# A chunked delta rule: inverses from blocks of 16 and a scan with its coefficients computed ahead

## Chip, cores and metric

The kernel runs on one core of a Trainium2 chip. The metric is device time in microseconds (us), the median of several runs. Five engines work from their own instruction queues: TensorE (PE, with its weight loads as PEld), VectorE (DVE), ScalarE (ACT), GpSimd (POOL) and SyncE (SP), which issues most DMAs.

## What is computed

Two blocks of two layers each act on 512 tokens of width 1024. The change touches the second block only, and in each of its two layers only the gated delta rule: 6 heads of width 64, run forwards and backwards over the tokens, in 8 chunks of 64 tokens. For each direction and head the reference does this:

```python
A = where(strict, einsum("bhncd,bhnsd->bhncs", kb, kc) * decay, 0)   # 64 x 64 in each chunk
u, w = triangular_solve(I + A, [vc * bc, kb * exp(gc)])              # unit lower triangular
Aqk  = einsum("bhncd,bhnsd->bhncs", qc, kc) * decay
qg, kdec, glast = qc * exp(gc), kc * exp(gc[-1] - gc), exp(gc[-1])
def step(state, ...):                                                # over the 8 chunks
    v_new = u_i - w_i @ state
    o     = qg_i @ state + aqk_i @ v_new
    state = state * gl_i + kdec_i.T @ v_new
```

In the same layer stand a convolution module (31 taps), a differential attention over 512 tokens (6 heads, 24 blocks of 128 queries) and the dense projections that feed all three. Their outputs meet in one output projection, and a feed-forward part follows.

## The kernel before

The kernel is written with tiles. A scheduler places the instructions of each engine in order when the kernel is compiled, earlier program text going first where several instructions are ready; on the chip each engine runs its list in that order. Tiles with the same tag share a fixed number of buffers, so a tile also waits for its buffer.

`second(l)` (L1959) is the layer. The six heads are taken in three pairs f, and each pair goes through five functions, whose calls stand between the dense projections in L2010 to L2037:

- `gates` makes the decays for all heads. At the end (L1377 to L1387) the decay of a whole chunk, `gl`, is made by writing each gate out over 64 columns (six tiles `gb`) and 24 matmuls of two columns (L1386).
- `delta_proj` projects and convolves q, k, v. `delta_prep` (L1418) makes the 64 x 64 products `L1` and `KK`, one for each direction, and writes them to DRAM (`gdd`).
- `delta_solve` (L1519) inverts the 32 x 32 diagonal blocks. A DMA brings one block to each partition; 31 steps of two DVE instructions on up to 256 columns do the substitution for all blocks at once (L1532 and L1534). It runs for pairs 0 and 1 together, after `prep(1)` (128 partitions), and for pair 2 alone (64 partitions). The inverse and its transpose return over DRAM (`xd`).
- `delta_uw` (L1543) takes 32-blocks to the 64 x 64 inverse `Z` by two products (L1577, L1586) and multiplies it with the values and keys (L1598) for `U` and `w_`; four transposes for each direction (L1604) give `wT`.
- `delta_scan` (L1610) steps through the 8 chunks in both directions: the state against `wT` (L1627) and `qT` (L1628), `vn` on DVE (L1630), then `kd` (L1636) and `Aq` (L1638) against `vn`, two DVE instructions for the state `S` (L1644), and a copy of the outputs by ACT (L1649). Each step and direction takes one of the two PSUM banks `sA`.
- `delta_out` (L1656) scales the part that came from the state, adds the parts of both directions, norms, and writes to `cat`.

`rest(f)` is `delta_prep2` (L1504), which makes what only the scan needs. The attention `diff` (L1779) stands after all of this in the program text and fills in between. `self.tt` and `self.mul` (L229) put an elementwise instruction on DVE or POOL by an estimate of their load; `self.evac` (L239) chooses ACT or DVE to empty a PSUM bank.

## Time and profile before

| what | value |
|---|---|
| median of 3 runs | 4081.32 us (4050.67 to 4096.1) |
| span of the profiled execution | 4073.4 us |
| the two stretches from the first gates to the output projection | 2262 to 2707 us and 3180 to 3628 us |

No separate time is listed for the profiled execution; its span lies 8 us under the median of the runs and inside their spread. Busy times are of one engine, and engines overlap. A matmul's end is modelled, and matmuls are pipelined, so the start of the next instruction tells more of what one costs than its duration. The granted clock of TensorE is a share of full speed; its two levels are 1.00 (2.4 GHz) and 0.50 (1.2 GHz), and a stretch that has both shows a mean.

### The profile page before, as it was taken

The page shows a single profiled execution, that of the slowest core. Times are in us where ns is not written, and L with a number is a line of the kernel's source. Part 1 is how long each engine was busy: PE and PEld are TensorE (multiplying, and loading weights), DVE is VectorE, ACT ScalarE, POOL GpSimd, SP SyncE. Part 2 cuts the span into 40 slices and gives each one's busy share as a digit, 9 for nine tenths or more (in the row PEclk, how much of TensorE's full clock was granted, in tenths as well). Part 3 has the DMA queues.
Part 4 walks back from the last instruction along what each step waited for, and adds up shares of the span by engine and source line. Part 5 has one row for each costly group of instructions (what it writes and reads, how often), then busy time and mean ns, then how long its engine had stood idle before and what let it go on. Part 6 is the DMA issues. An engine that isn't in the chain of part 4 may idle for free. (4 is left out here: it accounts for less than half of the span.)

```text
span 4073.4 us, 59952 instructions
## 1 busy us (share of the span) xinstructions
PE 3758.4 (92%) x23665; PEld 3302.7 (81%) x23665; DVE 2523.1 (62%) x4735; ACT 1601.9 (39%) x2702; POOL 1699.2 (42%) x1196
## 2 busy tenths in 40 slices
PE   8999989989998999998999978988999879988998
PEld 6888777989998888877999766778888766778988
DVE  6454566666556243337767595758667595758665
ACT  4544265332333222223434443534434444444433
POOL 2221234455452332234665453216654463216654
PEclk8999879999998999999999987769999887679999
DMA  6222444122221221222333334132333334132323
GB/s 206 86 81 77 154 139 146 42 63 67 69 73 65 70 70 62 70 62 57 98 104 103 114 95 122 45 117 101 105 100 112 101 97 124 40 117 101 107 95 113
DMA packets 419187, 384.06 MB, mean 94 GB/s; under 512 B 64586, under 2 KB 363865, under 8 KB 418009
## 3 DMA queue, kind: packets, MB, share of 16 engines
q1 hardware_dynamic: 413722, 370.95, 29.2%
q10 hardware_dynamic: 5183, 9.27, 0.8%
q8 instruction: 187, 3.06, 0.3%
q14 instruction: 95, 0.78, 0.1%
HBM read 335.35 MB, written 44.83 MB: 93 GB/s over the span
## 5 line engine op out<-in xcount | busy, mean ns | idle before, releaser
L232 POOL TENSOR_TENSOR wl<-raw,wh 128x1024 fp32r<-128x1024 f32 (+2 forms) x214 | 510.8, 2395 | 549.3 <-ACT wh L205 535.4
L205 ACT CAST wh<-raw 128x1024 fp32r<-128x1024 f32 (+2 forms) x441 | 444.4, 1013 | 642.3 <-PE mm L485 283.7
L232 DVE TENSOR_TENSOR wl<-raw,wh 128x1024 fp32r<-128x1024 f32 (+1 forms) x250 | 353.5, 1418 | 178.0 <-ACT wh L205 163.9
L484 PE MATMUL mm<-Hh,wh 128*128 128x512 f32 (+1 forms) x1256 | 417.6, 335 | 14.0 <-DVE x L1032 11.3
L486 PE MATMUL mm<-Hh,wl 128*128 128x512 f32 (+1 forms) x1256 | 416.9, 333 | 0.3 <-DVE wl L232 0.3
L485 PE MATMUL mm<-Hl,wh 128*128 128x512 f32 (+1 forms) x1256 | 416.7, 333 | 0.0
L484 PE MATMUL mm<-hh,wh 128*128 128x512 f32 (+1 forms) x640 | 238.5, 376 | 69.3 <-DVE dlo L1770 26.2
L484 PEld LDWEIGHTS mm<-Hh,wh 128*128 128x128 f32 x1256 | 238.6, 190 | 41.7 <-DVE x L1032 12.6
L486 PEld LDWEIGHTS mm<-Hh,wl 128*128 128x128 f32 x1256 | 238.7, 190 | 25.8 <-DVE wl L232 0.5
L485 PEld LDWEIGHTS mm<-Hl,wh 128*128 128x128 f32 x1256 | 239.0, 190 | 24.4
L486 PE MATMUL mm<-hh,wl 128*128 128x512 f32 (+1 forms) x640 | 234.0, 367 | 1.7 <-DVE wl L232 1.7
L485 PE MATMUL mm<-hl,wh 128*128 128x512 f32 (+1 forms) x640 | 233.2, 365 | 0.6 <-DVE hl L697 0.6
L508 PE MATMUL mm<-hl,wh 128*128 128x256 f32 (+1 forms) x808 | 226.2, 284 | 5.5 <-DVE hl L1945 5.4
L508 PE MATMUL mm<-hh,wl 128*128 128x256 f32 (+1 forms) x808 | 226.8, 285 | 4.8 <-DVE wl L232 4.4
L508 PE MATMUL mm<-hh,wh 128*128 128x256 f32 (+1 forms) x808 | 216.3, 285 | 6.5 <-ACT hh L1953 3.2
L205 ACT CAST wh<-s 128x1024 fp32r<-128x1024 f32 (+1 forms) x128 | 106.9, 835 | 269.4 <-PE mm L485 140.3
L484 PEld LDWEIGHTS mm<-hh,wh 128*128 128x128 f32 x640 | 127.8, 200 | 94.8 <-DVE dlo L1770 27.1
L508 PE MATMUL mm<-th,wh 128*128 128x256 f32 (+1 forms) x644 | 194.8, 304 | 8.1 <-ACT wh L205 5.6
L1032 DVE SCALAR_TENSOR_TENSOR x<-mm,mod,x 128x512 f32<-128x512 f32 (+1 forms) x224 | 138.0, 629 | 102.4 <-PE mm L486 101.8
L508 PE MATMUL mm<-th,wl 128*128 128x256 f32 (+1 forms) x644 | 196.2, 305 | 2.6 <-DVE wl L232 2.6
L508 PE MATMUL mm<-tl,wh 128*128 128x256 f32 (+1 forms) x644 | 194.7, 302 | 0.6 <-DVE tl L232 0.6
L232 POOL TENSOR_TENSOR Hl<-o,Hh 128x1024 fp32r<-128x1024 f32 (+3 forms) x76 | 140.5, 1850 | 94.4 <-ACT Hh L205 93.0
(763 smaller groups left out, 11023.1 us busy)
## 6 DMA issues: line engine op xcount, KB each, us to landing
raw<-in_w_ff_dram SPq DMA_DIRECT2D x68, 1024.0 KB
raw<-in_ffn_w_in_dram SPq DMA_DIRECT2D x88, 512.0 KB
raw<-in_mod_w_dram SPq DMA_DIRECT2D x40, 1024.0 KB
raw<-in_odd_w_in_dram SPq DMA_DIRECT2D x24, 1024.0 KB
raw<-in_ffn_w_out_dram SPq DMA_DIRECT2D x19, 1024.0 KB
raw<-in_w_in_dram SPq DMA_DIRECT2D x38, 512.0 KB
dqk<-qk SPq DMA_DIRECT2D x48, 256.0 KB
raw<-in_w_out_dram SPq DMA_DIRECT2D x12, 768.0 KB
```

The costliest lines, as they stand in the source:

```text
L205: nc.scalar.copy(hi, src)
L232: i = (nc.vector if e == "dve" else nc.gpsimd).tensor_tensor(out=out, in0=a, in1=b, op=op)
L484: mm(ps, ah, bh, start=first, stop=False)
L485: mm(ps, ah, bl, start=False, stop=False)
L486: mm(ps, al, bh, start=False, stop=last)
L508: i = self.nc.tensor.matmul(out, lhsT, rhs, start=start, stop=stop, skip_group_check=True)
L1032: self.nc.vector.scalar_tensor_tensor(out=x[:, ct, :n], in0=ps, scalar=gate[:, ct:ct + 1], in1=x[:, ct, :n], op0=ALU.mult, op1=ALU.add)
```

## The change

The diagonal blocks are inverted at size 16 instead of 32, for each pair by itself right after its `prep`: 15 steps of two DVE instructions on up to 64 columns, always on 128 partitions. `delta_uw` then goes from 16 to 32 by matmuls: for each pair and direction 32 products `pq` and 64 products `pz` of 32 x 32 blocks, with the masked tile `A16` before them, a multiplication or copy between them and a subtraction after them; the step from 32 to 64 stays.

The scan becomes a linear recurrence. `NM` (the chunk's decay on the diagonal less w against `kd`), the new part `pb` of each state and the coefficients `QT` of the outputs are computed for all chunks. A step is then two matmuls that add onto `pb` and one copy, on DVE for one direction and on ACT for the other. The outputs of both directions are summed in one PSUM bank at the end. The transposes `wT`, the tiles `S`, the output copies of each step and the sums in `delta_out` go. `gl` comes from two matmuls of 24 columns instead of 24 of two columns; `qg`, q times its decay, replaces the scaling in `delta_out`. The order of the calls in `second` stays.

```diff
...
+    same32 = i[:, None] % 64 // 32 == n64 // 32
+    dc[:, 3] = same32 & (i[:, None] % 32 < 16) & (n64 % 32 >= 16)
+    dc[:, 4] = same32 & (i[:, None] % 32 >= 16) & (n64 % 32 < 16)
+    c["dmc"] = dc.reshape(P, 320)
+    c["eye16"] = np.tile(np.eye(16).reshape(1, 256), (P, 1))
+    c["half"] = np.stack([i % 64 < 32, i % 64 >= 32, i % 32 < 16, i % 32 >= 16], 1)
...
+            mm(pg[:, 96 + 24 * d:120 + 24 * d], self.dm[:, 4], g[:, :, 6 * d:6 * d + 6], start=True, stop=True)
+        gc, egc, etl, beg, gl = T("gc"), T("egc"), T("etl"), T("beg"), T("gl")
         for d in range(2):
             sl = slice(6 * d, 6 * d + 6)
             v = lambda o: pg[:, o:o + 24].rearrange("p (a b) -> p a b", a=4)
             nc.vector.tensor_copy(gc[:, :, sl], v(24 * d))
             nc.scalar.activation(etl[:, :, sl], v(48 + 24 * d), AF.Exp)
+            nc.scalar.activation(gl[:, :, sl], v(96 + 24 * d), AF.Exp)
...
-        pg = self.psx()
-        for f in range(3):
-            for d in range(2):
-                gb = pool.tile([P, 4, P], F32, tag="E", name="gb", bufs=5)
-                src = g[:, :, 6 * d + 2 * f:6 * d + 2 * f + 2].unsqueeze(3).to_broadcast([P, 4, 2, 64])
-                self.tt(gb.rearrange("p t (h a) -> p t h a", h=2), src, self.ones4, 512, ALU.mult)
-                for tt in range(4):
-                    o = 16 * f + 8 * d + 2 * tt
-                    mm(pg[:, o:o + 2], gb[:, tt], self.dm[:, 4, 0:2], start=True, stop=True)
-        nc.scalar.activation(gl.rearrange("p f a b c -> p (f a b c)"), pg[:, :48], AF.Exp)
...
-        st = dict(KK=KK, gd=gd_, tk=tk, tv=tv)
-        if f == 0:
-            self.first = st
-        else:
-            self.delta_solve(l, [(0, 1), (2,)][f - 1], pool, [(self.first, st), (st,)][f - 1])
+        st = dict(KK=KK, tk=tk, tv=tv, xd=self.delta_solve(l, f, pool, gd_))
...
-        qT = st["qT"] = normed(1, tq)
-        products(qT, [(Aq[d], E["q", d]) for d in range(2)])
-        kd = []
+        products(normed(1, tq), [(Aq[d], E["q", d]) for d in range(2)])
+        kd, qg = [], []
         for d in range(2):
-            k = pool.tile([P, 4, 2, 64], F32, tag=f"kd{d}", name="kd", bufs=2)
-            self.tt(k, tk, gb("etl", d), 512, ALU.mult)
-            kd.append(k)
-        st.update(kd=kd, Aq=Aq)
+            for lst, t, n, tag in ((kd, tk, "etl", "kd"), (qg, tq, "egc", "qg")):
+                k = pool.tile([P, 4, 2, 64], F32, tag=f"{tag}{d}", name=tag, bufs=2)
+                self.tt(k, t, gb(n, d), 512, ALU.mult)
+                lst.append(k)
+        st.update(kd=kd, qg=qg, Aq=Aq)
...
+    def delta_solve(self, l, f, pool, gd):
+        nc = self.nc
+        g = pool.tile([P, 16, 16], F32, tag="chG", name="chG")
+        X = pool.tile([P, 16, 16], F32, tag="chX", name="chX")
+        tmp = pool.tile([P, 64], F32, tag="chT", name="chT")
+        nc.sync.dma_start(g, self.dview(gd, 0, [[1040, P], [64, 16], [1, 16]]))
+        nc.scalar.dma_start(X.rearrange("p a b -> p (a b)"), self.I["k_eye16"])
+        for j in range(15):
+            n, m = 15 - j, j + 1
             t = tmp[:, :n * m].rearrange("p (a b) -> p a b", a=n)
-            nc.vector.tensor_tensor(out=t, in0=g[:, j + 1:, j:j + 1].to_broadcast([L, n, m]),
-                                    in1=X[:, j:j + 1, :m].to_broadcast([L, n, m]), op=ALU.mult)
+            nc.vector.tensor_tensor(out=t, in0=g[:, j + 1:, j:j + 1].to_broadcast([P, n, m]),
+                                    in1=X[:, j:j + 1, :m].to_broadcast([P, n, m]), op=ALU.mult)
             nc.vector.tensor_tensor(out=X[:, j + 1:, :m], in0=X[:, j + 1:, :m], in1=t, op=ALU.subtract)
         nc.scalar.copy(g, X.rearrange("p a b -> p b a"))
-        for i, (f, st) in enumerate(zip(fs, sts)):
-            xd = self.p_dram.tile([2, 64, 1024], F32, tag=f"xd{l}{f}", name="xd")
-            nc.sync.dma_start(xd[0], X[64 * i:64 * i + 64].rearrange("p a b -> p (a b)"))
-            nc.sync.dma_start(xd[1], g[64 * i:64 * i + 64].rearrange("p a b -> p (a b)"))
-            st["xd"] = xd
+        xd = self.p_dram.tile([2, P, 256], F32, tag=f"xd{l}{f}", name="xd")
+        for x, t in enumerate((X, g)):
+            nc.sync.dma_start(xd[x], t.rearrange("p a b -> p (a b)"))
+        return xd
...
+        TZ = [pool.tile([P, 2, 8, 32], F32, tag=f"TZ{d}", name="TZ") for d in range(2)]
+        half = lambda i, n: self.half[:, i:i + 2].unsqueeze(1).unsqueeze(3).to_broadcast([P, n, 2, 512 // n // 2])
         for d in range(2):
+            raw = pool.tile([P, 2, 8, 16], F32, tag="Q", name="T16", bufs=2)
+            for x in range(2):
+                nc.sync.dma_start(raw[:, x], self.dview(xd, (x ^ d) * 32768 + 2048 * d, [[16, P], [4096, 8], [1, 16]]))
+            self.tt(TZ[d].rearrange("p x n (b j) -> p (x n) b j", b=2), raw.rearrange("p x n j -> p (x n) j").unsqueeze(2).to_broadcast([P, 16, 2, 16]),
+                    half(2, 16), 512, ALU.mult)
...
+            GI = pool.tile([P, 8, 64], F32, tag=f"GI{d}", name="A16")
+            self.mul(GI, KK.rearrange("p a b c -> p (a b) c"), self.dmc[:, 3 + d].unsqueeze(1).to_broadcast([P, 8, 64]), 512)
+            blocks = [(slice(32 * q, 32 * q + 32), n) for n in range(8) for q in range(4)]
+            pq = self.psx([P, 8, 32])
+            for b, n in blocks:
+                mm(pq[b, n], GI[b, n, b.start % 64:b.start % 64 + 32], T[b, n], start=True, stop=True)
+            A = pool.tile([P, 2, 4, 32], F32, tag="Q", name="AT", bufs=2)
+            if d == 0:
+                nc.vector.tensor_tensor(out=A, in0=pq.rearrange("p (h t) a -> p h t a", h=2),
+                                        in1=G["beta"][:, :, hs].rearrange("p t h -> p h t").unsqueeze(3).to_broadcast([P, 2, 4, 32]), op=ALU.mult)
+            else:
+                nc.vector.tensor_copy(A, pq.rearrange("p (h t) a -> p h t a", h=2))
+            A = A.rearrange("p h t a -> p (h t) a")
+            pz = self.psx([P, 2, 8, 32])
+            for b, n in blocks:
+                mm(pz[b, 0, n], TZ[d][b, 1, n], A[b, n], start=True, stop=True)
+                mm(pz[b, 1, n], A[b, n], TZ[d][b, 1, n], start=True, stop=True)
+            nc.vector.tensor_tensor(out=TZ[d], in0=TZ[d], in1=pz, op=ALU.subtract)
+            self.tt(Z.rearrange("p n (b j) -> p n b j", b=2), TZ[d][:, 1].unsqueeze(2).to_broadcast([P, 8, 2, 32]), half(0, 8), 512, ALU.mult)
...
-                self.evac(w_[:, tb], pu[:, :, :, 1], 256)
+                nc.scalar.activation(W[:, tb], pu[:, :, :, 1], AF.Copy, scale=-1.0)
...
-            pt = self.psx([P, 4, P])
-            for tt in range(4):
-                nc.tensor.transpose(pt[:, tt], w_[:, tt].rearrange("p a b -> p (a b)"), self.ident)
-            w = pool.tile([P, 4, P], F32, tag="E", name="wT", bufs=5) if f == 2 else pool.tile([P, 4, P], F32, tag=f"wT{d}", name="wT")
-            self.evac(w, pt, 512)
...
+        NM, SS, pbs, banks = [], [], [], []
+        for d in range(2):
+            gi = pool.tile([P, 4, 2, 64], F32, tag=f"GI{d}", name="GI")
+            self.tt(gi, G["gl"][:, :, hs(d)].unsqueeze(3).to_broadcast([P, 4, 2, 64]), eye, 512, ALU.mult)
+            NM.append(gi)
+        for d in range(2):
+            U, W, kd = (st[n][d] for n in ("U", "W", "kd"))
+            pb, b = psa.tile([P, 4, 2, 64], F32, tag="sA", name="sA"), self.bank()
+            for n in range(7):
+                tt, c = at(d, n)
+                for h in range(2):
+                    b(pb[half[1 - c], tt, h], kd[half[c], tt, h], U[half[c], tt, h], start=n < 2 and h == 0, stop=n == 0)
+            pn = self.psx([P, 4, 2, 64])
+            for tt, c, h in chunks:
+                mm(pn[half[c], tt, h], W[half[c], tt, h], kd[half[c], tt, h], start=True, stop=True)
+            nc.vector.tensor_tensor(out=NM[d], in0=pn, in1=NM[d], op=ALU.add)
+            SS.append(kd)
+            pbs.append(pb)
+            banks.append(b)
+        for n in range(7):
             for d in range(2):
+                tt, c = at(d, n)
+                t2, c2 = at(d, n + 1)
+                for h in range(2) if n else ():
+                    banks[d](pbs[d][half[c2], tt, h], NM[d][half[c], tt, h], SS[d][half[c], tt, h], start=False, stop=True)
+                if d == 0:
+                    nc.vector.tensor_copy(SS[d][half[c2], t2], pbs[d][half[c2], tt])
                 else:
+                    nc.scalar.copy(SS[d][half[c2], t2], pbs[d][half[c2], tt])
+        QT = []
+        for d in range(2):
+            W, Aq, qg = (st[n][d] for n in ("W", "Aq", "qg"))
+            pq, b = self.psx([P, 4, 2, 64]), self.bank()
+            for i, (tt, c, h) in enumerate(chunks):
+                b(pq[half[c], tt, h], qg[half[c], tt, h], self.ident[half[c], half[c]], start=tt == 0 and h == 0, stop=False)
+            for tt, c, h in chunks:
+                b(pq[half[c], tt, h], W[half[c], tt, h], Aq[half[c], h, tt], start=False, stop=True)
+            self.evac(qg.rearrange("p t a b -> p (t a b)"), pq.rearrange("p t a b -> p (t a b)"), 512)
+            QT.append(qg)
+        po, b = self.psx([P, 4, 2, 64]), self.bank()
+        for tt, c, h in chunks:
+            for d in range(2):
+                b(po[half[c], tt, h], st["Aq"][d][half[c], h, tt], st["U"][d][half[c], tt, h], start=tt == h == d == 0, stop=False)
+        for n in range(1, 8):
+            for d in range(2):
+                tt, c = at(d, n)
                 for h in range(2):
+                    b(po[half[c], tt, h], QT[d][half[c], tt, h], SS[d][half[c], tt, h], start=False, stop=True)
+        o = pool.tile([P, 4, 2, 64], F32, tag="OI", name="OI", bufs=2)
+        self.evac(o.rearrange("p a b c -> p (a b c)"), po.rearrange("p a b c -> p (a b c)"), 512)
+        return o
...
-        q = [OI[d][:, :, 0] for d in range(2)]
-        for d in range(2):
-            b = G["egc"][:, :, 6 * d + 2 * f:6 * d + 2 * f + 2].unsqueeze(3).to_broadcast([P, 4, 2, 64])
-            self.tt(q[d], q[d], b, 512, ALU.mult)
-            self.tt(q[d], q[d], OI[d][:, :, 1], 512, ALU.add)
-        o = pool.tile([P, 4, 2, 64], F32, tag="o2", name="oo", bufs=3)
-        self.tt(o, q[0], q[1], 512, ALU.add)
+        o = OI
```

## Rows read from the trace of the kernel before

**Rows 1.** The page: its span, and each engine's busy us, share and instructions.
```profile
span 4073.4 us, 59952 instructions
PE 3758.4 (92%) x23665; PEld 3302.7 (81%) x23665; DVE 2523.1 (62%) x4735; ACT 1601.9 (39%) x2702; POOL 1699.2 (42%) x1196
```

**Rows 2.** Stretches, two a layer: length, PE, PEld, DVE, ACT, POOL, clock, DMA, GB/s.
```profile
2262.00:2462.00 200.00, 166.47 (x908) 137.87 (x906) 146.88 (x242) 95.22 (x133) 111.33 (x71) 0.89 0.38 107
2462.00:2707.00 245.00, 209.50 (x1466) 164.01 (x1466) 170.20 (x534) 104.27 (x236) 51.67 (x49) 0.70 0.27 84
3180.00:3376.00 196.00, 162.44 (x876) 133.31 (x875) 144.09 (x241) 94.16 (x133) 111.43 (x71) 0.90 0.38 106
3376.00:3628.00 252.00, 219.24 (x1491) 169.50 (x1490) 173.34 (x537) 106.21 (x237) 54.60 (x48) 0.68 0.27 84
```

**Rows 3.** PE groups, 2262 to 2715: busy, mean ns, idle before, its releasers.
```profile
L484 PE MATMUL mm<-hh,wh 128*128 128x512 f32 x138 | 60.7, 446 | 31.9 <-DVE dlo L1770 12.2 <-ACT pk L242 7.0 <-DVE gg L1359 5.4
L1638 PE MATMUL sA<-vn,Aq 64*64 64x64 f32 x168 | 22.5, 268 | 1.0 <-DVE vn L1630 0.9
L1636 PE MATMUL sA<-vn,kd 64*128 64x128 f32 x72 | 22.1, 396 | 4.3 <-DVE vn L1630 4.3
L1386 PE MATMUL ax<-dm,gb 128*128 128x2 f32 x48 | 8.5, 314 | 0.0
```

**Rows 4.** DVE groups and one of ACT, 2262 to 2715, columns as in Rows 3.
```profile
L1532 DVE TENSOR_TENSOR chT<-chG,chX 128x31 f32<-128x31 f32 (+31 forms) x62 | 35.6, 574 | 1.4
L1534 DVE TENSOR_TENSOR chX<-chX,chT 128x31 f32<-128x31 f32 (+31 forms) x62 | 30.5, 491 | 1.2
L1644 DVE SCALAR_TENSOR_TENSOR S<-S,gl,sA 64x64 f32<-64x64 f32 x72 | 20.0, 278 | 15.9 <-PE sA L1638 14.8
L1630 DVE TENSOR_TENSOR vn<-U,sA 64x128 f32<-64x128 f32 x42 | 11.9, 285 | 5.6 <-PE sA L1628 4.6
L1455 DVE TENSOR_TENSOR gd<-ax,gc 128x512 f32<-128x512 f32 x6 | 4.1, 685 | 12.6 <-POOL eb L232 7.1 <-PE ax L1454 5.5
L1649 ACT COPY OI<-sA 64x256 f32<-64x256 f32 x42 | 15.4, 366 | 36.8 <-DVE S L1644 30.1 <-PE sA L1638 3.0 <-PE fx L1824 2.7
```

**Rows 5.** PE timeline, full clock: start, duration, line, tiles, shapes, count.
```profile
2332.23 0.98 PE L1483 MATMUL ax<-qT,kT 64*64 64x64 f32 x32
...
2454.97 0.21 PE L1577 MATMUL ax<-Tb,KK 32*32 32x32 f32 x1
...
2455.09 0.57 PE L1577 MATMUL ax<-Tb,KK 32*32 32x32 f32 x13
...
2585.49 0.43 PE L1627 MATMUL sA<-S,wT 128*64 128x128 f32 x2
2585.76 0.38 PE L1628 MATMUL sA<-S,qT 128*64 128x128 f32 x2
2586.08 0.55 PE L1850 MATMUL fx<-ident,dP 128*128 128x128 f32 x3
2586.55 0.69 PE L1577 MATMUL ax<-Tb,KK 32*32 32x32 f32 x16
...
2589.02 0.48 PE L1636 MATMUL sA<-vn,kd 64*128 64x128 f32 x2
2589.43 0.44 PE L1638 MATMUL sA<-vn,Aq 64*64 64x64 f32 x4
2589.80 0.50 PE L1824 MATMUL fx<-dqk 128*128 128x512 f32 x1
```

**Rows 6.** Two short stretches, columns as in Rows 2.
```profile
2580.00:2600.00 20.00, 20.00 (x228) 15.62 (x227) 14.42 (x46) 9.26 (x24) 4.21 (x4) 1.00 0.20 55
...
3490.00:3510.00 20.00, 20.00 (x109) 16.24 (x109) 13.27 (x40) 6.34 (x12) 1.34 (x2) 0.50 0.26 69
```

**Rows 7.** DVE timeline of the first substitution.
```profile
2400.89 2.38 DVE L1532 TENSOR_TENSOR chT<-chG,chX 128x175 f32<-128x175 f32 x1
...
2416.12 0.40 DVE L1532 TENSOR_TENSOR chT<-chG,chX 128x231 f32<-128x231 f32 x1
```

More of the change, by code (lines that the diff above doesn't have):

```diff
@@ L87, in shape_constants @@
     dm[:, 3] = same64 * (s < t)
-    dm[:, 4, 0] = i < 64
-    dm[:, 4, 1] = i >= 64
-    dm[:, 5] = same64
-    c["dm"] = dm.reshape(P, 768)
+    dm[:, 4] = same64
+    c["dm"] = dm.reshape(P, 640)
     n64 = np.arange(64)[None, :]
-    dc = np.zeros((P, 3, 64))
+    dc = np.zeros((P, 5, 64))
     dc[:, 0] = i[:, None] % 64 <= n64
@@ L1453, in delta_prep @@
             pr = self.psx([P, 4, 2, 64])
-            mm(pr, self.dm[:, 5], gd, start=True, stop=True)
+            mm(pr, self.dm[:, 4], gd, start=True, stop=True)
             nc.vector.tensor_tensor(out=gd, in0=pr, in1=gb("gc", d), op=ALU.subtract)
@@ L1470, in delta_prep @@
                 pr = self.psx([P, 4, 2, 64])
-                mm(pr, self.dm[:, 5], eb, start=True, stop=True)
+                mm(pr, self.dm[:, 4], eb, start=True, stop=True)
                 nc.vector.tensor_tensor(out=eb, in0=pr, in1=e, op=ALU.mult)
@@ L1529, in delta_solve @@
-        for j in range(31):
-            n, m = 31 - j, j + 1
+        g = pool.tile([P, 16, 16], F32, tag="chG", name="chG")
[5 more added lines that the diff above has]
+            n, m = 15 - j, j + 1
             t = tmp[:, :n * m].rearrange("p (a b) -> p a b", a=n)
-            nc.vector.tensor_tensor(out=t, in0=g[:, j + 1:, j:j + 1].to_broadcast([L, n, m]),
-                                    in1=X[:, j:j + 1, :m].to_broadcast([L, n, m]), op=ALU.mult)
+            nc.vector.tensor_tensor(out=t, in0=g[:, j + 1:, j:j + 1].to_broadcast([P, n, m]),
+                                    in1=X[:, j:j + 1, :m].to_broadcast([P, n, m]), op=ALU.mult)
@@ L1546, in delta_uw @@
         mm = nc.tensor.matmul
[L1547 removed]
+        st["U"], st["W"] = [], []
         xd = st["xd"]
         Zs = [pool.tile([P, 8, 64], F32, tag=f"Z{d}", name="Z") for d in range(2)]
[L1550 removed]
+        TZ = [pool.tile([P, 2, 8, 32], F32, tag=f"TZ{d}", name="TZ") for d in range(2)]
+        half = lambda i, n: self.half[:, i:i + 2].unsqueeze(1).unsqueeze(3).to_broadcast([P, n, 2, 512 // n // 2])
         for d in range(2):
[L1552 to L1557 removed]
+            raw = pool.tile([P, 2, 8, 16], F32, tag="Q", name="T16", bufs=2)
[3 more added lines that the diff above has]
+                    half(2, 16), 512, ALU.mult)
         VBs = []
@@ L1589, in delta_uw @@
             U = pool.tile([P, 4, 2, 64], F32, tag="E", name="U", bufs=5) if f == 2 else pool.tile([P, 4, 2, 64], F32, tag=f"U{d}", name="U")
-            w_ = pool.tile([P, 4, 2, 64], F32, tag="w_", name="w_", bufs=1)
+            W = pool.tile([P, 4, 2, 64], F32, tag="E", name="W", bufs=5) if f == 2 else pool.tile([P, 4, 2, 64], F32, tag=f"W{d}", name="W")
             for b in range(2):
@@ L1652, in delta_scan @@
-        self.load["dve"] += 8000
-        self.load["act"] += 6000
-        return OI
+        half = [slice(0, 64), slice(64, 128)]
+        at = lambda d, n: divmod(n if d == 0 else 7 - n, 2)
+        hs = lambda d: slice(6 * d + 2 * f, 6 * d + 2 * f + 2)
+        eye = self.dmc[:, 2].unsqueeze(1).unsqueeze(1).to_broadcast([P, 4, 2, 64])
+        chunks = [(tt, c, h) for tt in range(4) for c in range(2) for h in range(2)]
+        NM, SS, pbs, banks = [], [], [], []
[3 more added lines that the diff above has]
+            NM.append(gi)
@@ L1875, in second_consts @@
         T = lambda n, s: pool.tile(s, F32, tag=n, name=n)
-        self.dm = T("dm", [P, 6, P])
-        nc.scalar.dma_start(self.dm, I["k_dm"].rearrange("p (a b) -> p a b", a=6))
-        self.dmc = T("dmc", [P, 3, 64])
-        nc.scalar.dma_start(self.dmc, I["k_dmc"].rearrange("p (a b) -> p a b", a=3))
-        self.half = T("half", [P, 2])
+        self.dm = T("dm", [P, 5, P])
+        nc.scalar.dma_start(self.dm, I["k_dm"].rearrange("p (a b) -> p a b", a=5))
+        self.dmc = T("dmc", [P, 5, 64])
+        nc.scalar.dma_start(self.dmc, I["k_dmc"].rearrange("p (a b) -> p a b", a=5))
+        self.half = T("half", [P, 4])
         nc.scalar.dma_start(self.half, I["k_half"])
-        self.ones4 = self.ones.unsqueeze(1).to_broadcast([P, 4, P]).rearrange("p t (h a) -> p t h a", h=2)
         for n, src, rows in (("cw", "delta_conv_w_2", 54), ("dw", "conv_dw_w_2", 124)):
@@ L1977, in second @@
         pool = p_dl.enter_context(tc.tile_pool(name=f"dl{l}", bufs=1))
-        self.S = [[pool.tile([P, P], F32, tag=f"S{p}{d}", name="S") for d in range(2)] for p in range(2)]
-        for p in self.S:
-            for t in p:
-                nc.gpsimd.memset(t, 0.0)
         def park(dst, act=None):
```

69 lines of the change are left out of this document (8 added, 61 removed).

## The prediction

> **What bounds the kernel now.** I read the page first: TensorE is busy for 92% of the span and no other engine is near it [rows 1]. That average hides the part that changes, so I next took the busy times by stretch. In each layer of the second block, the part from the first gates to the output projection falls in two [rows 2]. In the first stretch (A, 200 and 196 us) the dense projections run, at a clock of 0.89. In the second (B, 245 and 252 us) scans, the last solve and the attention share the engines, at 0.70. TensorE is covered for 166 of 200 us in A and 210 of 245 in B. DVE has 147 and 170.
>
> The reader is to see two different limits here. In A the list of PE groups shows what TensorE waits for: 12.2 us for `dlo` on DVE and 7.0 us for an ACT copy, of 31.9 in front of L484 [rows 3]. Both fall while DVE works off the substitution, which stands ahead of `dlo` in its queue; ACT holds its place for the same reason. So about 19 us of A is DVE's substitution seen from TensorE. In B, short stretches show TensorE without a gap at both clocks: 228 instructions in 20 us at 1.00, 109 in 20 us at 0.50 [rows 6]. So in B TensorE is itself a limit, at the clock that it is granted, and idle for 35 us besides. DVE there is about two thirds busy. The groups of ACT and DVE show the scan as a chain in which each engine waits for the next: the output copy waits 30.1 us for `S`, and `S` 15.9 us for TensorE [rows 4].
>
> I therefore count TensorE in us at full clock. Covered time by clock gives 148 + 147 = 295 for the first layer, 146 + 149 = 295 for the second [rows 2]. Time is then 295 divided by the mean clock (0.785 over both stretches) plus 69 us of idle: 445 us (the second layer: 66 idle, 448).
>
> **The change, part by part: DVE and ACT.** The substitution goes: 35.6 + 30.5 us for 124 instructions, 0.53 each [rows 4]. In its place come 90 (3 pairs, 15 steps, 2), of 15 to 64 columns. Such a size isn't in the trace's rows; 231 columns take 0.40 [rows 7]. I bound one by 0.11 (columns in proportion) and 0.53 (today's mean), and take 0.3, since a small instruction doesn't shrink in proportion: 27 us (10 to 48). The scan loses `S` and `vn`, 31.9 us [rows 4]. Added on DVE: for each pair and direction a subtraction and a sum of 512 columns from PSUM at 0.69, as L1455 [rows 4], and one of 256 at half of that, 10 us a layer; and 21 state copies of the shape of `vn`, 0.285 at most, 6 us. Elementwise work of 512 columns that can go to POOL grows by 24 instructions (`A16`, one more mask, `gi`, `qg`) and loses 21 (15 in `delta_out`, 6 `gb`): nothing. DVE in all: 98 off, 43 on, so 317 becomes about 262 a layer. ACT loses 15.4 us of output copies [rows 4] for 21 state copies. Neither is an end by itself; what it takes away are waits.
>
> **TensorE, removed.** At full clock, a scan step in one direction costs, start to next start, 0.27 (L1627), 0.32 (L1628), 0.41 (L1636) and 0.37 (L1638) [rows 5]: 1.37 us. Fourteen steps, two first steps without the state's products and two last without `kd`, are 20 us a pair, 60 a layer. The gates' 48 two-column instructions are 8.5 us [rows 3] and the 24 transposes cost 0.16 each like L1850 [rows 5], 3.8 us. Sum: 72 off.
>
> **TensorE, added.** A float32 product is two instructions, as in these rows. From 16 to 32 they are 64 for `pq` and 128 for `pz`, for each pair and direction. Sixteen at one place of the array take 0.69 us, 43 ns each; where two places alternate, six start in 0.12 us (2454.97 to 2455.09), 20 ns each [rows 5]. `pq` changes place with every product, so 20 ns; `pz` with every second, so 31 between the two. That is 5.3 us, times 6: 32 us (23 to 50). The new scan has 416 instructions of 64 x 64 a pair (56 `pb`, 64 `pn`, 48 steps, 128 `QT`, 120 outputs). L1483 alternates places, 32 in 0.98 us, 31 ns; L1638 is four at one place in 0.37 us, 93 ns, with a wait in front [rows 5]. The new loops have two products at a place before they change, so I take the middle, 62 ns: 26 us a pair, 77 a layer (39 to 115). The two matmuls for `gl` are nothing beside that.
>
> So TensorE's work isn't reduced: 295 - 72 + 32 + 77 = 332 us a layer at full clock (285 to 388). A gain must come from idle time and from the clock.
>
> **Idle time.** The solve of pair 0 no longer waits for pair 1, so `uw(0)`, `scan(0)` and `uw(1)`, which stand ahead of the last dense projections in the text, can run in A, with dense matmuls to fill the waits. The 19 us in front of `dlo` and the copy go, as three solves of 30 short instructions replace one of 62. In B the ping-pong of a step falls from four changes of engine to two (two matmuls, a copy), and everything else in a scan runs for all chunks without a wait. I take 10 us for this, of the idle time that `vn` and `S` put in front of TensorE. 69 becomes 40.
>
> The new waits: a step's matmuls wait for a copy, one direction on DVE, one on ACT, where it is queued behind the attention's exponentials; attention matmuls queued behind them on PE wait too. Both `sA` banks are held for a whole scan, so `scan(1)` starts its `pb` after the last copy of `scan(0)`; steps hand them on today. SP's queue: three reads of blocks, six writes of `xd` and twelve reads of it, as before, with half the bytes; a write that waits for a solve still holds the weight loads behind it, but for a shorter solve. I put both at nothing, covered by the dense work of A; uncovered, one trip over DRAM is late in B for pair 2 only.
>
> **The clock and the sum.** A after: 148 - 8 + two `uw` at 20 (10.6 new; 128 instructions of L1577 and L1586 at 39 ns; 64 of L1598, twice the columns of L1483, 4 us) + one scan 26 = 206, at 0.90: 229 us. B: 332 - 206 = 126 at a clock between 0.70 (today) and 1.00 (where many small matmuls stand ready [rows 6]); the middle, 0.85: 148 us. With 40 idle: 417 us, against 445 and 448, so 28 + 31 = 59 us less. The sum is made against the profiled execution (4073 us); I take it off the median of the runs: **4022 us**. The runs spread over 1.1%, so about 1% is what a measurement can tell from no change.
>
> **The rivals.**
> *TensorE at today's clock takes it all back.* B's clock stays at 0.70: 126 / 0.70 = 180, total 449, and nothing changes: 4086 us. For it: gapless 20 us at 0.50 [rows 6], and the added work is of the small kind that runs there. Against: B loses work to A and waits less.
>
> *Slower: the small products cost what L1638 costs.* At 93 ns the scans take 115 instead of 77. Place: the products `QT` and `po` in both stretches. A 219 / 0.90 = 243, B 151 / 0.70 = 216, idle 40: 499 us, 4186 us. At that clock it decides from about 73 ns each. For it: the row itself; against: four instructions behind a wait are a poor measure of a long run, and L1483 is at 31.
>
> *Faster: B at full clock.* The chain was what starved TensorE, its runs get long, and B takes 126 us with 30 idle in all: 385 us, 3958 us. For it: 228 instructions in 20 us at 1.00. Against: at 0.50 TensorE had no gap either, and the clock didn't rise [rows 6]. The Trainium skill, "TensorE: Matmul & The Clock Gate", Part 1, says that the throttle is the default and that activity releases it, which would give this result. The trace agrees only in part: covered time alone didn't release it in 3490 to 3510.
>
> *The substitution stays slow.* Eight instructions of 175 to 220 columns start between 2400.89 and 2416.12, 1.9 us each, where 231 columns take 0.40 right behind [rows 7]; POOL is busy for 111 of 200 us in A [rows 2]. Were the 60 instructions of pairs 0 and 1 held like that, they would take 114 us, DVE would fill A, and the 19 us would stay, with some 2 more: 417 + 21 = 438 us, 4064 us. The Trainium skill, "SBUF — State Buffer", Who interferes with whom, says that a DVE instruction with two SBUF inputs contends with a POOL instruction that reads SBUF, and is blocked for the whole of it. By that rule the price goes by the number of instructions, not their columns, and the number falls only from 124 to 90. The trace agrees in those eight instructions; most of the 124 show no such hold.
>
> **How the numbers follow.** Forecast 0.36; B at full clock 0.18; today's clock 0.26; slow substitution 0.06; small products at 93 ns 0.14. Faster by over 1% (under 4040): 0.54. Within 1%: 0.32. Slower: 0.14. The forecast's own range is 4000 to 4045. The whole range has to take in the full clock (3958, with something under it for idle) and today's clock with part of the price bound: 3945 to 4125, which leaves out most of the slowest case.
>
> **What would show it.** DVE: L1532 and L1534 gone, 90 short ones under 30 us; DVE's busy time down by about 55 us a layer. TensorE: no 12 us in front of L484, `pq` and `pz` near 5 us for each direction, a scan's products near 26 us, and the first `pb` well before the last dense projection. The clock of the last part of the stretch at 0.85. I am wrong if TensorE's covered time in these stretches grows, if the first scan still starts after the dense part, or if the steps are still some us apart because copies queue behind the attention.

## The result and the profile after

The changed kernel takes 4026.17 us (median; 4024.1 to 4036.42) beside 4080.88 us of the kernel before: a ratio of 0.989, 95% interval 0.984 to 0.994 (the two medians alone give 0.987). The prediction was 4022 us. The profiled executions have spans of 4034.6 and 4073.4 us. The number was near; most terms of the sum that led to it were not, and they cancelled, which is luck.

The page of the kernel after, engine by engine (busy us, share of the span, instructions), beside [rows 1]:

```profile
PE 3704.7 (92%) x27441; PEld 3287.6 (81%) x27441; DVE 2440.8 (60%) x4507; ACT 1571.0 (39%) x2654; POOL 1669.0 (41%) x1168
```

The stretches that answer to [rows 2], busy times, granted clock (PEclk), DMA share and GB/s of the kernel after:

```profile
2266.00:2458.00 192.00, 171.21 (x1393) 141.35 (x1393) 138.76 (x259) 94.42 (x140) 103.00 (x69) 0.92 0.41 112
2458.00:2688.00 230.00, 179.10 (x2871) 151.16 (x2868) 135.14 (x403) 90.93 (x206) 49.06 (x43) 0.72 0.26 82
3165.00:3357.00 192.00, 169.68 (x1414) 139.64 (x1412) 138.39 (x259) 95.72 (x144) 105.27 (x70) 0.95 0.42 115
3357.00:3586.00 229.00, 178.11 (x2854) 150.14 (x2854) 133.97 (x403) 89.62 (x202) 46.71 (x40) 0.70 0.26 80
```

Line numbers of the two kernels differ by up to 16. The reader is to see that TensorE has twice the instructions in B and less covered time, and that B's clock is what it was. Covered time by clock gives 286 us a layer at full clock, where before it was 295 and the prediction had 332 (the finer slices of the table below put the fall at 14 us). Idle time is 72 us in the first layer, where the prediction had 40.

For all kernels below one table is used. It counts each layer from the first matmul of the gates' decays to the first of the output projection; covered time by clock is summed over slices of 10 us. The two numbers in a cell are the two layers.

| kernel | ratio to before (95%) | stage, us | TensorE at full clock, us | idle, us |
|---|---|---|---|---|
| before | 1 | 416.8, 419.1 | 279.7, 279.0 | 63.6, 60.7 |
| after | 0.989 (0.984 to 0.994) | 393.6, 392.3 | 266.1, 265.4 | 68.4, 69.3 |
| solve alone | 1.011 (1.006 to 1.015) | 447.7, 435.7 | 289.7, 293.8 | 51.9, 51.2 |
| scan alone | 0.993 (0.991 to 0.995) | 396.6, 397.3 | 255.9, 251.9 | 85.7, 83.7 |
| no substitution | 0.986 (0.982 to 0.990) | 380.5, 383.0 | 265.9, 266.0 | 65.1, 62.9 |
| three times `pn` | 0.993 (0.990 to 0.996) | 398.4, 393.0 | 276.8, 278.7 | 71.0, 71.7 |
| fill attention | 1.012 (1.009 to 1.014) | 425.4, 433.9 | 279.5, 279.2 | 73.3, 73.5 |
| fill, twice | 1.019 (1.016 to 1.021) | 448.9, 450.1 | 298.9, 296.6 | 80.7, 75.9 |
| solve alone, filled | 1.029 (1.026 to 1.033) | 469.0, 476.1 | 313.4, 311.5 | 61.5, 56.4 |
| scan(2) late | 0.991 (0.988 to 0.993) | 392.3, 390.6 | 267.8, 267.8 | 67.1, 67.6 |
| `QT` by addition | 0.986 (0.984 to 0.988) | 388.6, 381.0 | 262.8, 262.1 | 69.9, 70.7 |
| both of these | 0.988 (0.985 to 0.990) | 389.6, 391.5 | 264.1, 263.5 | 68.6, 72.6 |
| solve books 18 | 0.996 (0.995 to 0.998) | 402.5, 404.5 | 270.3, 270.7 | 74.4, 78.1 |
| solve books 0, scan(2) late | 0.989 (0.986 to 0.992) | 395.0, 385.2 | 264.5, 266.8 | 77.9, 74.7 |

The kernel before had medians of 4061 to 4081 us in the sessions, so ratios are compared, not medians.

### The profile page after: what moved, and what is told of

It is laid out like the page before. It is cut to its first block, busy times and chain, and to the rows that moved or that the text cites. A ratio compares the mean times of both kernels' runs of the same rounds, so it can differ in the third digit from the quotient of the medians.

```text
span 4034.6 us, 67160 instructions
## 1 busy us (share of the span) xinstructions
PE 3704.7 (92%) x27441; PEld 3287.6 (81%) x27441; DVE 2440.8 (60%) x4507; ACT 1571.0 (39%) x2654; POOL 1669.0 (41%) x1168
## 5 line engine op out<-in xcount | busy, mean ns | idle before, releaser
L233 POOL TENSOR_TENSOR wl<-raw,wh 128x1024 fp32r<-128x1024 f32 (+2 forms) x196 | 468.1, 2397 | 530.7 <-ACT wh L206 476.5
L233 DVE TENSOR_TENSOR wl<-raw,wh 128x1024 fp32r<-128x1024 f32 (+1 forms) x268 | 378.1, 1415 | 189.1 <-ACT wh L206 176.4
L509 PE MATMUL mm<-hl,wh 128*128 128x256 f32 (+1 forms) x808 | 231.5, 290 | 6.4 <-DVE hl L1960 6.3
L509 PE MATMUL mm<-hh,wl 128*128 128x256 f32 (+1 forms) x808 | 231.6, 290 | 5.5 <-DVE wl L233 4.1
L509 PE MATMUL mm<-hh,wh 128*128 128x256 f32 (+1 forms) x808 | 218.4, 288 | 6.5 <-ACT hh L1968 3.2
L509 PE MATMUL mm<-th,wh 128*128 128x256 f32 (+1 forms) x644 | 195.3, 305 | 8.1 <-ACT wh L206 5.5
L509 PE MATMUL mm<-th,wl 128*128 128x256 f32 (+1 forms) x644 | 197.3, 307 | 3.1 <-DVE wl L233 3.1
L509 PE MATMUL mm<-tl,wh 128*128 128x256 f32 (+1 forms) x644 | 195.3, 303 | 0.6 <-DVE tl L233 0.6
L509 PEld LDWEIGHTS mm<-hl,wh 128*128 128x128 f32 (+1 forms) x808 | 155.8, 193 | 9.7 <-DVE hl L1960 7.7
```

Source lines behind the costliest of these rows:

```text
L233: i = (nc.vector if e == "dve" else nc.gpsimd).tensor_tensor(out=out, in0=a, in1=b, op=op)
L509: i = self.nc.tensor.matmul(out, lhsT, rhs, start=start, stop=stop, skip_group_check=True)
```

## Experiments: one part of the change at a time

**Solve alone.** The kernel before with the new `delta_solve` and the doubling in `delta_uw`:

```diff
...
-            self.delta_solve(l, [(0, 1), (2,)][f - 1], pool, [(self.first, st), (st,)][f - 1])
+        st = dict(KK=KK, tk=tk, tv=tv, xd=self.delta_solve(l, f, pool, gd_))
...
```

> The kernel before with the new solve only (blocks of 16 for each pair by itself, doubled by matmuls); the old scan with its wT, S and vn stays. Theory 1 (the solve's waits in the dense part were worth something, but the old scan still ends the stage): the 12 us and 7 us waits of TensorE in the dense part go, scan(0) starts about as late as before, and the scan's chain still runs until the output projection: 5 to 12 us a layer, 4057 to 4070 us. Theory 2 (the solve carries the gain, since pair 0 no longer waits for pair 1): at least 20 us a layer, 4040 us or less. Theory 3 (the added products and DVE work eat the waits saved): within 5 us of 4081.

It took 4108 us, ratio 1.011: slower, which none of the three theories had. On PE, the first product of `uw(2)` and the starts of the two directions of scan(2), of the kernel before:

```profile
2586.55 0.69 PE L1577 MATMUL ax<-Tb,KK 32*32 32x32 f32 x16
...
2623.46 0.49 PE L1636 MATMUL sA<-U,kd 64*128 64x128 f32 x2 [0.58 <-ACT OI L1649]
...
2625.31 0.79 PE L1636 MATMUL sA<-U,kd 64*128 64x128 f32 x2 [0.70 <-ACT OI L1649]
```

The same three in the solve alone:

```profile
2587.58 0.57 PE L1570 MATMUL ax<-TZ,A 32*32 32x32 f32 x42
...
2636.70 0.79 PE L1653 MATMUL sA<-U,kd 64*128 64x128 f32 x2
...
2656.75 0.48 PE L1653 MATMUL sA<-U,kd 64*128 64x128 f32 x2
```

`uw(2)` begins at the same time, the first direction of scan(2) 13 us later and the second 31 us later. The doubling puts two more trips from TensorE to DVE and back ahead of each `U`, here in a stretch where the queues hold the steps of scan(1) and the attention. The old scan(2) takes some 65 us from there and is the last chain to end (the last `vn` stands at 2692 us before, at 2721 here), so the stage of this layer ends 29 us later. TensorE's work rose by 10 and 15 us a layer (the doubling), and idle time fell by 12 and 10, as the solve's waits went.

The clock is a rival to this account. The part after the dense matmuls in the solve alone, both layers, columns as in [rows 2]:

```profile
2469.00:2736.00 267.00, 237.81 (x2123) 185.82 (x2119) 162.45 (x506) 99.94 (x229) 45.50 (x46) 0.61 0.22 72
3414.00:3672.00 258.00, 226.51 (x2129) 177.81 (x2128) 164.87 (x508) 100.45 (x229) 45.98 (x44) 0.66 0.23 75
```

Beside B in [rows 2], TensorE is covered for 28 and 7 us longer and idle for no longer, and covered time by clock is the same (145 and 149 us, against 147 and 149). In these rows the loss of this part is the lower clock, 0.61 and 0.66 instead of 0.70 and 0.68. Whether the longer chain brought the clock down or the lower clock stretched the chain isn't shown.

**Scan alone.** The kernel after with the old substitution on blocks of 32 for pairs 0 and 1 together, and no doubling:

```diff
...
-        st = dict(KK=KK, tk=tk, tv=tv, xd=self.delta_solve(l, f, pool, gd_))
...
+            self.delta_solve(l, [(0, 1), (2,)][f - 1], pool, [(self.first, st), (st,)][f - 1])
...
```

> The changed kernel with the old solve (blocks of 32, pairs 0 and 1 together, no doubling by matmuls from 16); the new scan, gl and outputs stay. Theory 1 (the shorter scan carries most of the gain): 14 to 20 us a layer, 4040 to 4053 us, with the scans' steps 15 to 20 us long as in the changed kernel and the 12 us wait in front of the dense matmuls back. Theory 2 (the solve carries it): 4060 us or more. If the two parts add up, this run's gain and that of the solve alone sum to about 55 us.

Ratio 0.993, 28 us of 4061, and 20 and 22 us a layer in the profile: theory 1. The parts don't add up: +0.011 and -0.007 against -0.011 together. With the new scan the longer `uw` costs nothing that shows, which fits scans that are short and a last one that no longer ends the stage: with the new solve and the new scan, `uw(2)` starts at 2576 and the last scan is done by 2630.

**No substitution.** The kernel after, its 30 DVE instructions a pair left out:

```diff
-        for j in range(15):
-            n, m = 15 - j, j + 1
...
```

> The changed kernel without its 90 substitution instructions a layer (the block's inverse is left at the identity; all else is issued as before), so 32 us of DVE a layer and the latency of each solve go. Theory 1 (DVE still holds the dense part back, since it is busy for 139 of its 192 us): 8 to 15 us a layer, 3996 to 4010 us. Theory 2 (the substitution is hidden by the dense matmuls now): within 8 us of 4026. Both leave the last part of the stage, after 2458 us, as it is.

Ratio 0.986. The profile gives 13 and 9 us a layer, theory 1's size; the ratios give 14 us in all, between the two theories, with intervals that overlap. Up to the last dense matmul the stages are 6 and 5 us shorter. The other 7 and 5 lie behind it, which the expectation left as it was; pair 2's substitution stands there among the state copies of scan(0), on DVE from 2487.90 to 2495.70 us in the kernel after. The groups of DVE after, 2254 to 2690 us (count, busy us and mean ns, idle before), show more:

```profile
L1518 DVE TENSOR_TENSOR chT<-chG,chX 128x15 f32<-128x15 f32 (+7 forms) x45 | 16.5, 367 | 4.0 <-DMA chG<-gdd 3.4
L1520 DVE TENSOR_TENSOR chX<-chX,chT 128x15 f32<-128x15 f32 (+7 forms) x45 | 15.5, 345 | 0.8
...
L1650 DVE COPY kd<-sA 64x128 f32<-64x128 f32 x21 | 6.1, 288 | 10.2 <-PE sA L509 10.1
...
L1638 DVE TENSOR_TENSOR GI<-ax,GI 128x512 f32<-128x512 f32 x6 | 4.1, 689 | 2.4 <-PE ax L1637 2.3
```

Of the 90 instructions 76 take 15.4 us, 0.20 each. The other 14 take 0.91 to 2.32 us each, 16.7 us in all, whatever their size:

```profile
2370.41 1.27 DVE L1518 TENSOR_TENSOR chT<-chG,chX 128x15 f32<-128x15 f32 x1
...
2402.16 1.06 DVE L1520 TENSOR_TENSOR chX<-chX,chT 128x63 f32<-128x63 f32 x1
```

All 14 overlap a POOL instruction in time, and of the 76 only 6 do. That is the hold of [rows 7] again, half of the substitution's time. The Trainium skill, "SBUF — State Buffer", Who interferes with whom, gives the rule: DVE's second pair of ports is shared with GpSimd and locked by one of them. The trace agrees here.

**Solve books 18.** `self.load["dve"] += 6000` becomes 18000, which moves later elementwise work from DVE to POOL and ACT.

> The changed kernel with the load that the solve books for DVE raised from 6 to 18 (thousand) for each pair, so that elementwise work after it goes to POOL and ACT instead of DVE. No work is added or removed. Theory 1 (DVE holds the dense part, as taking the substitution away gained 5 to 7 us a layer): some us of DVE leave the dense part, 2 to 6 us a layer less, 4014 to 4022 us. Theory 2 (POOL takes longer for the same instructions, and what waits for them comes later): within 3 us a layer or up to 8 us a layer more, 4020 to 4042 us.

Ratio 0.996, 9 and 12 us a layer lost, most of it idle time (74 and 78 us): theory 2, beyond its bound of 8. POOL instructions take longer (with 512 columns in the solve alone, `OI` took POOL 1.43 us and DVE 0.69) and, by the hold above, may slow DVE's as well; which of the two was not told apart.

## Experiments: what the last part hangs on

**Three times `pn`, and fill.** The same kind of work in two places. In the scan:

```diff
-            for tt, c, h in chunks:
+            for tt, c, h in chunks * 3:
                 mm(pn[half[c], tt, h], W[half[c], tt, h], kd[half[c], tt, h], start=True, stop=True)
```

> The changed kernel with the products pn (w against kd) issued three times in a row into the same bank, which adds 128 instructions for each pair and direction, 768 a layer, at the 40 ns that one takes in the changed kernel's trace: 31 us of TensorE at full clock a layer, and nothing for any other engine. Theory 1 (TensorE is itself the limit of the last part, at the clock of 0.72 that it was granted): 31 / 0.72 = 43 us a layer for two thirds of them at least, 4085 to 4112 us. Theory 2 (engines wait for each other there, and TensorE has 51 us of idle time): under 10 us a layer, below 4046 us. Theory 3 (more small products raise the granted clock): between the two, with a clock above 0.72 in the last part.

In the attention, ahead of each block's transposes, where they are overwritten:

```diff
+            for i in range(8):
+                for q in range(4):
+                    r = slice(32 * q, 32 * q + 32)
+                    nc.tensor.matmul(pt[r, i % 4, 32 * (i // 4):32 * (i // 4) + 32], pe[r, 0, 32 * i:32 * i + 32],
+                                     pe[r, 0, 32 * i:32 * i + 32], start=True, stop=True)
```

> The changed kernel with 32 more products of 32x32 in each of the attention's 24 blocks, just ahead of the block's transposes and into the same bank, which the transposes then overwrite: 64 instructions a block at the 12 ns that pq takes in the changed kernel's trace, 18 us of TensorE at full clock a layer. Nothing else is added. Theory 1 (the last part of the stage is TensorE at a granted clock of 0.72, and dense runs of small products raise it, as the stretches of scans at 1.00 suggest): the clock of the last part rises to 0.85 or more, (129 + 18) / 0.85 = 173 us covered instead of 179, so 3 to 10 us a layer less, 4005 to 4022 us. Theory 2 (the clock does not follow): 18 / 0.72 = 25 us a layer more, about 4075 us. Theory 3 (the work fits into TensorE's idle 51 us): 4018 to 4034 us at an unchanged clock.

> As the run with 32 more products in each attention block, with 64: 36 us of TensorE at full clock a layer. Theory 1 (the clock follows the small products): the clock nears 1.00, (129 + 36) / 0.97 = 170 us covered, 4 to 9 us a layer less than the changed kernel, 4008 to 4020 us. Theory 2: 50 us a layer more, about 4126 us. Theory 3 (idle time takes it, until it is used up): 4030 to 4060 us.

The expectation counted the added `pn` twice. The 16 products of a pair and direction are 32 instructions, so two more rounds add 64, and 384 a layer (a layer's trace has 576 `pn` instead of 192): 15 us at 40 ns, not 31. They added 11 and 13 us of work, 28 to 34 ns each, and cost 5 and 1 us. That is theory 2's time but not its mechanism, since idle time didn't take the work: it rose by 3 and 2 us. The clock rose, as theory 3 has it. The part after the dense matmuls with three times `pn` (two rows, one a layer), then with the fill:

```profile
2456.00:2696.00 240.00, 186.43 (x3291) 159.07 (x3290) 134.66 (x404) 91.56 (x207) 48.34 (x43) 0.75 0.26 80
3360.00:3594.00 234.00, 179.68 (x3291) 153.70 (x3290) 135.08 (x403) 91.30 (x207) 48.02 (x41) 0.78 0.26 82
...
2454.00:2721.00 267.00, 210.98 (x4443) 178.53 (x4442) 135.06 (x404) 94.56 (x207) 47.90 (x43) 0.69 0.23 72
3384.00:3657.00 273.00, 218.99 (x4441) 185.57 (x4440) 135.06 (x403) 94.07 (x207) 47.65 (x41) 0.66 0.22 70
```

The kernel after has 0.72 and 0.70 there. The fill added 13 and 14 us, about as much, and cost 32 and 42. Idle time took 5 and 4 of that; the rest is TensorE's covered time, some 9 and 13 us of it for the lower clock (an estimate from these rows: 211 us less 211 times 0.69 / 0.72, and 219 less 219 times 0.66 / 0.70). Twice the fill, 33 and 31 us of work, ran at 0.73 and 0.70, about the clock of the kernel after, and cost 55 and 58, with 12 and 7 us more of idle time. So the clock followed the small products in the scans and not in the attention, and theory 2 was too low for one fill and near for two. The same amount of work costs more in the attention than in a scan; how much of that is the clock and how much the attention's own chain isn't separated.

The attention's tail shows its chain. Transposes of four blocks in the kernel after, where the clock is 0.50, and the end of the stage:

```profile
2655.75 1.11 PE L1866 MATMUL fx<-ident,dP 128*128 128x128 f32 x4 [0.37 <-DVE dmx L1842]
...
2661.00 1.11 PE L1866 MATMUL fx<-ident,dP 128*128 128x128 f32 x4 [0.73 <-POOL dP L1860]
...
2665.10 1.05 PE L1866 MATMUL fx<-ident,dP 128*128 128x128 f32 x4
...
2669.17 1.06 PE L1866 MATMUL fx<-ident,dP 128*128 128x128 f32 x4
...
2682.95 1.12 PE L1707 MATMUL mm<-ident,do 128*128 128x128 f32 x4 [10.07 <-POOL do L233]
2687.53 2.50 PE L485 MATMUL mm<-hh,wh 128*128 128x512 f32 x5 [3.46 <-DVE hh L208]
```

With the fill, in its tail, where one block ran at full clock:

```profile
2644.45 0.75 PE L1868 MATMUL fx<-dP 32*32 32x32 f32 x64
2645.14 0.66 PE L1871 MATMUL fx<-ident,dP 128*128 128x128 f32 x4
...
2647.90 1.10 PE L509 MATMUL mm<-dv,dat 128*128 128x64 f32 x8 [1.87 <-ACT dat L243]
...
2649.91 1.09 PE L1871 MATMUL fx<-ident,dP 128*128 128x128 f32 x4
...
2654.10 1.08 PE L1868 MATMUL fx<-dP 32*32 32x32 f32 x64
2655.11 1.11 PE L1871 MATMUL fx<-ident,dP 128*128 128x128 f32 x4
```

Blocks are 4.1 to 5.3 us apart in the kernel after, at half clock. With the fill the one at full clock takes 4.8 us, 0.7 of it the fill, and TensorE waits 1.87 us for ACT's copy instead. So the pace of this block is that of its round through PE, DVE and ACT, and twice the clock hardly shortens it. One block doesn't show that the clock costs little in the whole tail, and `QT` by addition, below, speaks against it.

During the scans the attention stands still. Busy time of the scores' matmuls alone (L1840, two a block), the stretches of the kernel after:

```profile
2455.00:2484.00 29.00, 3.18 (x6) 1.28 (x6) 0.69 0.57 169
2484.00:2503.00 19.00, 0.00 (x0) 0.00 (x0) 0.67 0.15 29
2503.00:2556.00 53.00, 8.06 (x14) 3.27 (x14) 0.70 0.20 56
2556.00:2570.00 14.00, 0.00 (x0) 0.00 (x0) 0.92 0.06 23
2570.00:2613.00 43.00, 8.15 (x16) 3.27 (x16) 0.88 0.16 54
2613.00:2630.00 17.00, 0.00 (x0) 0.00 (x0) 0.90 0.12 43
2630.00:2671.00 41.00, 7.85 (x12) 3.33 (x12) 0.58 0.34 115
```

The three stretches with no scores are the scans, 14 to 19 us each; the 24 blocks fill the rest, six of them after the last scan.

**Solve alone, filled.** The same fill in the solve alone, to see whether its loss was B's clock:

> The new solve with the old scan (108 us... 4108 us before this edit), with the same 32 products in each attention block. Theory 1 (the new solve with the old scan is slow because the last part runs at a clock of 0.55 to 0.67, not because of its work): the clock rises, and the time falls to 4090 us or less. Theory 2 (it is slow because of added work and waits): 4108 to 4155 us, as 18 us a layer come on top.

4182 us, 1.029: theory 2, and more than it allowed. The clock after the dense matmuls was 0.67 and 0.64, beside 0.61 and 0.66 without the fill. It rose in one layer alone, and not far, so this run doesn't tell whether a higher clock would give the loss back.

**Scan(2) late.**

```diff
-        scan(2)
-        self.level(0, 0, 100)
-        out(2)
         self.level(*BAL[2])
+        self.late = lambda: (scan(2), out(2))
...
             outputs(b)
+            if b == 18:
+                self.late()
```

> The changed kernel with scan(2) and out(2) called in the attention's loop after block 18 of 24, so that the attention goes first until then. Theory 1 (the last 58 us of the stage are attention alone, at a clock of 0.50, so scan work beside it costs little there): 4 to 10 us a layer less, 4006 to 4018 us. Theory 2 (scan(2) and out(2) become the end of the stage, as in the kernel before): 5 to 15 us a layer more, 4036 to 4056 us.

Ratio 0.991, and 1.3 and 1.7 us off the stages: neither theory. The attention comes last in both kernels; scan(2) ends 40 us before the stage does, instead of 59 and 61. Where it stands among the blocks makes little difference, which fits that one stands still while the other runs.

**`QT` by addition.** The products with the identity also turn q times its decay; here it is added unturned, so the kernel leaves out a transposition and no longer computes the layer.

```diff
...
-            for i, (tt, c, h) in enumerate(chunks):
-                b(pq[half[c], tt, h], qg[half[c], tt, h], self.ident[half[c], half[c]], start=tt == 0 and h == 0, stop=False)
...
+            nc.vector.tensor_tensor(out=qg, in0=pq, in1=qg, op=ALU.add)
```

> The changed kernel with QT made of 32 instructions for each pair and direction instead of 64: the products with the identity, which bring q times its decay into the bank, go, and one addition on DVE takes the place of the copy that empties the bank. TensorE loses 192 instructions a layer at 40 ns, 7.7 us at full clock; DVE gets 6 additions of 0.69 us for copies that were shared between ACT and DVE. Theory 1 (the time of the stage is TensorE's work over its granted clock plus its idle time): 7.7 / 0.72 = 10.7 us a layer less if all of it is in the last part, 4 to 11 us a layer, 4004 to 4018 us. Theory 2 (such work fills TensorE's idle time, as most of the repeated pn did): within 2 us a layer, 4022 to 4030 us. Theory 3 (the additions wait in DVE's queue and hold the scans' outputs): up to 5 us a layer more.

> QT by addition and scan(2) late together. If the two are worth what they are alone, the gains add up: about 3 us a layer for the late scan, and 4 to 11 us for QT by theory 1, so 3998 to 4012 us. If TensorE's idle time takes it, 4018 to 4026 us.

Ratios 0.986 and 0.988. Alone the stages lost 5 and 11 us for 3.3 us less work: theory 1's size, more than the work taken away. In the second layer all of it lies behind scan(2), where the attention, `out(2)` and the end of the convolution are left. The kernel after, then `QT` by addition:

```profile
3525.00:3585.00 60.00, 39.00 (x163) 32.37 (x161) 32.33 (x107) 24.63 (x48) 4.84 (x4) 0.52 0.36 123
...
3508.00:3556.00 48.00, 26.31 (x148) 22.11 (x147) 30.91 (x105) 23.38 (x44) 4.86 (x4) 0.68 0.46 153
```

TensorE's idle time is 21 and 22 us, and its covered time is shorter at a higher clock. In the first layer this stretch is 59 us in both kernels. No run shows why the clock differs. With the late scan most of the gain was gone, so gains of this size depend on the order that results, and on the clock that comes with it.

**The solve books nothing, scan(2) late.** The line `self.load["dve"] += 6000` goes.

> The changed kernel with scan(2) and out(2) after block 18 of the attention, and with no load booked for the solve, the opposite of the run that booked 18 and became 25 us slower, 10 us a layer, mostly of TensorE's idle time. Theory 1 (work moved from DVE to POOL is late, so less of it on POOL is better): some us of the dense part's idle time go, 3 to 8 us a layer less than with scan(2) late alone (0.991 of the kernel before), 0.987 or less. Theory 2 (the booked 6 already lies near the best point, as DVE is full from 2340 to 2400 us): within 0.002 of 0.991, or slower, as DVE gets more of the dense part's work and the first solves come later.

0.989: theory 2. No run with all of the computation beat the changed kernel by more than the intervals.

## Why the prediction was right, and where it was not

**TensorE removed and added: two terms were too dear.** On PE after, with L1559 as `pq`, L1569 and L1570 as `pz`, L509 as the scan's products:

```profile
2432.56 0.75 PE L1559 MATMUL ax<-TZ,A 32*32 32x32 f32 x64
2433.24 1.14 PE L509 MATMUL sA<-U,kd 64*64 64x64 f32 x28
2434.31 0.50 PE L487 MATMUL mm<-hh,wl 128*128 128x512 f32 x1
...
2436.85 0.27 PE L1569 MATMUL ax<-AT,TZ 32*32 32x32 f32 x7
...
2438.24 0.50 PE L485 MATMUL mm<-hh,wh 128*128 128x512 f32 x1
...
2500.92 2.17 PE L509 MATMUL ax<-kd,qg 64*64 64x64 f32 x56
2503.02 0.75 PE L1559 MATMUL ax<-TZ,A 32*32 32x32 f32 x64
```

From start to next start, `pq` is 64 in 0.68 us and `pz` 128 in 1.39: 2.1 us, not 5.3, so 12 a layer, not 32. The scan's products are 28 in 1.07 and 56 in 2.10, 38 ns, not 62; over both layers their seven kinds have means of 24 to 38 ns at full clock. That is 41 to 47 us a layer, not 77. The end nearer L1483's 31 ns [rows 5] was the right one. With these two the prediction's own sum is 295 - 72 + 12 + 47 = 282 (276 with 41), against 286 measured. The single parts agree to a few us: the scan alone lost 24 and 27 us (-72 + 47 is -25), the solve alone gained 10 and 15 (12). So the 72 removed was right to a few us.

**Idle time: the solve's half was right, the scan's had the wrong sign.** The prediction took 19 us off for the solve and 10 for the scan. Taken with the new scan, the solve is worth 17 and 14 us of idle time (scan alone against after), and the 12.2 and 7.0 us in front of L484 [rows 3] are gone. What A waits for now is, from the list of PE's waits, 2254 to 2460 us (total us, times, longest):

```profile
PE mm L485 <- DVE pc L1394: 8.9, 3, 6.8
PE ax L1583 <- DVE TZ L1571: 3.0, 1, 3.0
PE mm L486 <- DVE wl L233: 2.8, 1, 2.8
```

The scan alone raised idle time by 22 and 23 us, against a fall of 10 in the sum. It takes work off TensorE, and while a scan runs the attention gives it nothing else to do (the stretches with no scores above). 69 became 72, not 40.

**Scan(0) in A: wrong.** Its `pb` did start in A (2433.24), but its steps ran from 2484, after the dense part. From the kernel after, DVE's next-to-last `dlo`, the first `pn`, the first state copy, and the busy times (columns as in [rows 2]) of a stretch before the copy:

```profile
2451.92 0.69 DVE L1786 SCALAR_TENSOR_TENSOR dlo<-mm,dhi 128x512 fp32r<-128x512 f32 x1 [7.21 <-DMA qk<-dhi]
...
2479.37 0.36 PE L1637 MATMUL ax<-kd,W 64*64 64x64 f32 x1
...
2481.82 0.29 DVE L1650 COPY kd<-sA 64x128 f32<-64x128 f32 x1
...
2440.00:2463.00 23.00, 21.40 (x189) 16.27 (x187) 3.88 (x8) 5.81 (x11) 5.10 (x5) 1.00 0.59 173
```

`pn`, the first copy and `NM` (2482.15) stand in the orders of TensorE and DVE behind the last dense work, `prep(2)` and the first attention blocks. Up to 2463 DVE wasn't full: it was busy for 3.9 of 23 us, and its order waited at `dlo` for the DMA of the `dhi` before it. So the first scan started after the dense part, one of the prediction's signs of being wrong. Of the other two, covered time fell (376 to 350 us in the first layer), and the steps of scan(0) took 15 us, as its copies stood among pair 2's substitution, those of the others 6 and 9. TensorE was covered for 171 us in A, where the prediction had 229, and for 179 in B, where it had 148.

**B's clock: wrong.** 0.72 and 0.70, where the forecast took 0.85 and one rival today's 0.70. The rival was right on the clock, and failed by the same 46 us of work too many. The Trainium skill, "TensorE: Matmul & The Clock Gate", Part 1, says that activity releases the throttle. The runs agree in part: three times `pn` raised the clock after the dense matmuls from 0.72 and 0.70 to 0.75 and 0.78, and the fill, about as much work, lowered it to 0.69 and 0.66. Why the clock falls where it does stays open.

**DVE.** Less by 43 us a layer, not 55. The substitution took 32 us and not 27, by the 14 held instructions; state copies (6.1) and the sums on `GI` and `TZ` (8.2) were as counted. Most of the rest is a term that the prediction put at nothing: the change also books less load for DVE, so more elementwise work stays there. `wl` takes it 20.3 us in 17 instructions, where it was 9.2 in 8, and POOL has 11 us less. The slow rival had the right mechanism, but for 14 of 90 instructions at 1.2 us each, where it took 60 at 1.9. The rivals of 93 ns and of full clock are both out: 38 ns, 0.72.

So the total came out by luck: TensorE's work was put 46 us too high, idle time 32 too low and the mean clock too high. What carries the gain is the new scan, 20 and 22 of the 23 and 27 us a layer. With it TensorE has 25 us less of work and 22 more of idle time, and scan(2) no longer ends the stage. Whether the work or the shorter chain gives the gain isn't separated: 11 and 13 us of work put back into the scans cost only 5 and 1, at a higher clock. The new solve is worth 3 and 5 us a layer beside it by the profiles (the intervals of the two ratios overlap), and alone made the kernel slower.

## To carry to other kernels

Add up the price of a change where it stands: 11 to 14 us of small products cost 1 to 5 us in the scans and 32 to 42 us inside the attention, and the granted clock moved up with the one and down with the other. Look at the clock of a stretch before you put a loss down to its chain. Price a new kind of product by the longest gapless run of its nearest kind, not by the few behind a wait. When two parts of a change are bundled, run each alone: one was a loss whose cost the other hid.
